# Seven-product blocks: partial sums that grow in PSUM, and quarter-weight sums made by adding transfers

## The chip, the cores and the metric

The kernel runs on one core of one Trainium2 chip. The metric is device microseconds (us) of one execution, the median over several runs. The engines are named as in the profile: PE (TensorE matmul), PEld (its weight load), DVE (VectorE), ACT (ScalarE), POOL (GpSimd) and SP (SyncE, which here only issues transfers). SBUF is the on-chip memory that all engines read and write; PSUM is the small memory into which PE adds up its products.

## The reference, cut to what matters

One layer of a hybrid model is computed for 1152 tokens (1024 of a prompt and 8 x 16 of a sample) with 1024 channels. The attention and the state-space scan in the middle are not touched by the change. It touches the three last matrix products, of which two are meant here: the attention projection and the output projection.

```python
att_branch = (o_att.reshape(b, s, ATT_WIDTH) * jax.nn.silu(z_att)) @ w_att_proj     # 1024 x 1024
...
ssd_branch = y @ w_ssd_proj                                                         # 2048 x 1024
g_att, g_ssd = jnp.split(gates, 2, axis=-1)
merged = jax.nn.sigmoid(g_att) * att_branch + jax.nn.sigmoid(g_ssd) * ssd_branch
out = x + gate * (merged @ w_out)                                                   # 1024 x 1024
```

## The kernel before, in words

Everything lies with channels on the 128 partitions and tokens along the columns. A matrix product in float32 precision is made of float16 parts: an operand x is split into hi = x rounded to float16 (made on ACT) and lo = x - hi (made on DVE), and a product is hi*hi + hi*lo + lo*hi, three matmuls that add up in the same PSUM bank. `halves` (L637, L638) makes the two parts, `level` (L629) adds a sum of squares of the raw operand on ACT, from which a `verdict` at the end decides on the chip whether the general version has to run after all.

The two projections are done in blocks by a scheme with seven products instead of eight (as in Strassen's and Winograd's methods). A block takes two output tiles of 128 channels (o = 0, 1), both halves of the tokens (t = 0, 1, 576 tokens each) and inputs in pairs of 128-channel tiles (k = 0 to 3, e = 0, 1). So weights and inputs are 2 x 2 arrays of quarters. Four sums or differences of quarter weights and four of quarter inputs are made first; seven products of quarters follow, and sums of these give the four output quarters. There are eight blocks: four for the attention projection, with the four phases of the state-space projection (`ssd_dense`) behind them, and then four for the output projection.

- `job` lists the weight loads in the order of use; `w_ahead` (L619) loads them on SP's queue into three raw places of 1024 columns. `quad_split(i)` makes the float16 weights of block i: it takes its two raw tiles, makes the four sums on DVE (L661 to L664, 512 columns each) in two tiles u, splits w[0], u[0], half of w[1] and u[1], and calls `level` on the raw tiles. `w_next(i)` is called twice within block i and makes the weights of block i + 1 when there is room.
- `pieces` makes the four input sums (L2154 to L2157) and all float16 parts (L2140 on ACT, L2142 on DVE) of one pair of input tiles.
- `quad_dense` runs a block. `product(q, banks)` issues 4 x 2 x 3 = 24 matmuls (L782 to L784), each 128 x 128 weights by 288 columns, into two banks. The banks rotate over the three PSUM pools s (one place of two banks), g (three banks) and d (three banks), a fresh pair for each product. Products come in the order 0, 1, 5, 6, 4, 3, 2. ACT copies product 0 to SBUF (L817), and DVE adds the others to partial sums in SBUF (`joined`, L796). In the first block of each projection (`wide`) the products 0, 1 and 2 run together, k by k, since the inputs of the last k arrive late.
- `evict(o, t, y)` takes one output quarter from SBUF: for the attention projection it multiplies by a gate row (L2218), for the output it scales, adds x and stores it (L2308, L2311, L2312, L2313). `verdict()` is called in the last block, at evict(1,1).
- `gate_loads` (L2189) fetches the 16 gate rows from memory on SP's queue, up to five ahead of the one in use. POOL's queue carries stores, among them those of the gate rows (L1823), and POOL computes a small chain (from L1306).
- All places in SBUF come from one arena with fixed layouts (`L_TAIL` "T" are places of 1152 columns, `L_WQ` of 512 words for weights). `alloc` raises `NoSlot` if no place is free, and the generator that asked tries later.

The program is first emitted by generators, one per activity, and `run` interleaves these by their estimated time. Then `Order` puts every engine's instructions in a fixed order: it simulates the engines with a cost for each instruction (a transfer issued by POOL 0.56 us, plus 2.1 us and its bytes) and takes, on each engine, the earliest emitted instruction that is ready, of those that are ready with a margin first. On the chip each engine runs its list in this order and waits where an input is not there yet.

Of the kernel before, what the change touches and what calls it, by code (L numbers as in the profile page):

```python
# [16 lines left out]
P = 128  # L17
# [403 lines left out]
def trunk_kernel(ctx: ExitStack, tc: tile.TileContext, h, again):  # L421
# [217 lines left out]

    def quad_split(i):  # L640

        w_ahead()
        w = [wraw[j] for j in jobs[i]]
        bufs = []
        try:
            for _ in range(7):
                bufs.append(alloc(L_WQ, "w", 1024))
            for _ in range(2):
                bufs.append(alloc(L_TAIL, "T", 1024))
# [4 lines left out]
        u = bufs[7:]  # L654
        del bufs[7:]
        for j in jobs[i]:
            wraw.pop(j)
        a, b = ([x.ap.rearrange("p (k e m) -> p e k m", e=2, m=P)[:, e] for e in range(2)] for x in w)
        t = [x.ap.rearrange("p (e k m) -> p e k m", e=2, m=P)[:, e] for x in u for e in range(2)]
        halves(bufs[0].r, bufs[1].r, w[0].ap, SW)  # L660
        nc.vector.tensor_tensor(t[0], b[0], b[1], ALU.add)  # L661
        nc.vector.tensor_tensor(t[1], t[0], a[0], ALU.subtract)  # L662
        nc.vector.tensor_tensor(t[2], a[0], b[0], ALU.subtract)
        nc.vector.tensor_tensor(t[3], a[1], t[1], ALU.subtract)  # L664
        k4 = lambda x: x.rearrange("p (k m) -> p k m", m=P)
        halves(bufs[3].r, bufs[4].r, u[0].ap, SW)
        halves(k4(bufs[2].r[:, :512]), k4(bufs[2].r[:, 512:]), b[1], SW)
# [6 lines left out]
        nat = lambda k, e: slice((2 * k + e) * P, (2 * k + e + 1) * P)  # L674
        col = lambda k, e: slice((4 * e + k) * P, (4 * e + k + 1) * P)
        pick = {0: (bufs[0], bufs[1], nat, 0, 0), 1: (bufs[0], bufs[1], nat, 1, 1), 2: (bufs[5], bufs[6], col, 1, 1),
# [75 lines left out]
    for i in range(0, 8, 2):  # L752
        job(h["watt"][i], h["watt"][i + 1], quad=True)
# [4 lines left out]
    for i in range(0, 8, 2):  # L758
        job(h["wout"][i], h["wout"][i + 1], quad=True)

    HT = NT // 2
    HC = NT // 4

    def quad_dense(ops, evict, last=False, wide=False):

        i = widx[0]
        widx[0] += 1
        _, w = yield from w_wait(i)
        used, begun = {}, set()

        def product(q, banks, ks=range(4)):
            if q in begun:
                return
            for k in ks:
# [5 lines left out]
                for g, ps in enumerate(banks):  # L780
                    c = slice(g * HC, (g + 1) * HC)
                    nc.tensor.matmul(ps, wh, xh[:, c], start=k == 0, stop=False)  # L782
                    nc.tensor.matmul(ps, wh, xl[:, c], start=False, stop=False)  # L783
                    nc.tensor.matmul(ps, wl, xh[:, c], start=False, stop=k == 3)  # L784
                    yield 3 * 122.0
# [6 lines left out]
        def joined(t, banks, op):  # L792
            y = yield from walloc(L_TAIL, "T", HT)
            for g, ps in enumerate(banks):
                c = slice(g * HC, (g + 1) * HC)
                nc.vector.tensor_tensor(y.ap[:, c], t.ap[:, c], ps, op)  # L796
            return y

        def bank(n):
            if n % 3 == 0:  # L800
                x = pss.tile([P, 2, 512], F32, tag="s", name=nm("s"))
                return [x[:, g, :HC] for g in range(2)]
            if n % 3 == 1:
# [3 lines left out]
        b = bank(0)  # L807
        if wide:
            qs = (0, b), (1, bank(1)), (2, bank(2))
# [3 lines left out]
            begun.update((0, 1, 2))  # L813
        yield from product(0, b)
        s1 = yield from walloc(L_TAIL, "T", HT)
        for g, ps in enumerate(b):
            nc.scalar.activation(s1.ap[:, g * HC:(g + 1) * HC], ps, AF.Copy)  # L817
        if wide:
            p3 = yield from walloc(L_TAIL, "T", HT)
            for g, ps in enumerate(qs[2][1]):  # L820
                nc.scalar.activation(p3.ap[:, g * HC:(g + 1) * HC], ps, AF.Copy)
        b = qs[1][1] if wide else bank(1)
        yield from product(1, b)
        c = yield from joined(s1, b, ALU.add)
        yield from evict(0, 0, c) or ()
        b = bank(2)
        yield from product(5, b)
# [3375 lines left out]
```

## Time and profile before

| | |
|---|---|
| time, median of 3 runs | 1734.88 us (1734.16 to 1736.05) |
| span of the profiled execution, first to last instruction | 1732.7 us |
| mean granted clock of TensorE | 0.998 |
| PE busy | 1706.9 us (99%) |
| DVE, ACT, POOL busy | 1294.7, 982.9, 314.4 us (75%, 57%, 18%) |
| transfers | 287.26 MB, mean 166 GB/s |

The profile is of one execution. Its own time outside the span is not recorded; the span stands 2.2 us below the median of the runs. In the groups, "x48 | 19.9, 450 | 20.4" means 48 instructions, 19.9 us busy in all, 450 ns each, and 20.4 us in which the engine was idle just before one of them, with what ended that idleness behind the arrow. In the timeline the first number is the start in us and the second the duration; matmuls overlap, so 0.29 us each are issued every 0.12 us.

### The profile page before, as it was taken

What the parts mean: (1) busy time and instruction counts of PE and PEld (TensorE: products, weight loads), DVE (VectorE), ACT (ScalarE), POOL (GpSimd) and SP (SyncE); (2) the same over time, 40 slices, a digit from 0 to 9 for tenths busy, and PEclk for the clock granted to TensorE, in tenths of its full rate; (3) what the DMA queues carried; (4) which work ended last, traced back from release to release, by engine and by line L of the source; (5) the groups of instructions that cost most, each with busy time, mean ns of one, the idle gap of its engine ahead of it and who ended that gap; (6) DMA issues with size and microseconds to landing.
All of it is one profiled execution on the core that took longest, in us unless ns stands there. A gap on an engine that the chain in (4) does not pass through costs nothing. (4 is left out here: it accounts for less than half of the span.)

```text
span 1732.7 us, 35395 instructions
## 1 busy us (share of the span) xinstructions
PE 1706.9 (99%) x13977; PEld 1094.3 (63%) x13977; DVE 1294.7 (75%) x2449; ACT 982.9 (57%) x1931; POOL 314.4 (18%) x576
## 2 busy tenths in 40 slices
PE   7999999999999999999999999999999999999998
PEld 3556566566555566667666666666666677666676
DVE  6458767878776876587869777777777878897694
ACT  8766556566465646566556545755567543365340
POOL 0243233225134011111311231112112200000000
PEclk9999999999999999999999999999999999999999
DMA  9248789887978586445655445544556646331141
GB/s 383 80 126 206 174 229 214 183 228 192 214 210 197 150 203 140 138 137 150 150 153 155 139 134 162 169 136 118 152 174 223 252 157 226 118 127 51 53 160 71
DMA packets 276777, 287.26 MB, mean 166 GB/s; under 512 B 209069, under 2 KB 209721, under 8 KB 276601
## 3 DMA queue, kind: packets, MB, share of 16 engines
q1 hardware_dynamic: 267640, 256.26, 53.7%
q0 software_dynamic: 8960, 28.65, 4.5%
q8 instruction: 111, 1.82, 0.5%
q14 instruction: 66, 0.53, 0.1%
HBM read 192.70 MB, written 43.66 MB: 136 GB/s over the span
## 5 line engine op out<-in xcount | busy, mean ns | idle before, releaser
L873 PE MATMUL d<-arena 128*128 128x384 f16 x1872 | 610.9, 326 | 2.8 <-ACT arena L1707 1.4
L876 PE MATMUL d<-arena 128*128 128x384 f16 x1872 | 610.3, 326 | 0.0
L874 PE MATMUL d<-arena 128*128 128x384 f16 x1872 | 610.3, 326 | 0.0
L873 PEld LDWEIGHTS <-arena 128*128 128x128 f16 x1896 | 185.5, 98 | 127.6 <-issue 13.6
L876 PEld LDWEIGHTS <-arena 128*128 128x128 f16 x1896 | 185.5, 98 | 122.6
L874 PEld LDWEIGHTS <-arena 128*128 128x128 f16 x1896 | 185.6, 98 | 117.2 <-issue 3.2
L629 ACT ACTIVATE arena<-arena 128x1024 bf16<-128x1024 f32 (+4 forms) x185 | 184.9, 999 | 106.1 <-DMA arena<-in_wall_dram 64.8
L638 DVE SCALAR_TENSOR_TENSOR arena<-arena 128x1024 f16<-128x1024 f32 (+2 forms) x133 | 159.6, 1205 | 75.5 <-ACT arena L637 72.7
L637 ACT ACTIVATE arena<-arena 128x1024 f16<-128x1024 f32 (+2 forms) x133 | 135.7, 1022 | 90.8 <-DVE arena L662 18.7
L926 PE MATMUL d<-arena 128*128 128x384 f16 (+1 forms) x568 | 186.8, 329 | 0.0
L928 PE MATMUL d<-arena 128*128 128x384 f16 (+1 forms) x568 | 186.1, 328 | 0.0
L927 PE MATMUL d<-arena 128*128 128x384 f16 (+1 forms) x568 | 186.1, 328 | 0.0
L1472 ACT ACTIVATE arena<-arena 128x640 f32<-128x640 f32 (+4 forms) x144 | 100.8, 701 | 62.7 <-DVE arena L1475 62.2
L1918 ACT ACTIVATE arena<-arena 128x128 f32<-128x128 f32 x288 | 89.4, 392 | 39.5 <-DMA arena<-acs_d 38.8
L1730 DVE SCALAR_TENSOR_TENSOR arena<-arena 128x1176 f32<-128x1176 f32 x72 | 104.0, 1445 | 3.3 <-issue 1.3
L926 PEld LDWEIGHTS <-arena 128*128 128x128 f16 x576 | 56.3, 98 | 50.8 <-issue 17.5
L1508 DVE SCALAR_TENSOR_TENSOR arena<-arena 128x640 f16<-128x640 f32 (+4 forms) x128 | 86.8, 711 | 0.0
L1367 ACT ACTIVATE arena<-d 128x256 f32<-128x256 f32 x71 | 26.9, 378 | 96.4 <-PE d L928 96.4
L928 PEld LDWEIGHTS <-arena 128*128 128x128 f16 x576 | 56.4, 98 | 38.4 <-issue 0.2
L927 PEld LDWEIGHTS <-arena 128*128 128x128 f16 x576 | 56.4, 98 | 32.8
L1475 DVE CUSTOM_DVE_ANT_0 arena<-s,arena 128x320 f32<-128x320 f32 (+4 forms) x128 | 60.2, 501 | 19.8 <-PE s L1637 9.8
L1400 POOL TENSOR_SCALAR arena<-arena 128x16 f32<-128x16 f32 (+1 forms) x24 | 10.0, 417 | 353.8 <-DVE arena L1373 353.6
(267 smaller groups left out, 3051.7 us busy)
## 6 DMA issues: line engine op xcount, KB each, us to landing
arena<-in_wall_dram SPq DMA_DIRECT2D x85, 512.0 KB, 4.7
arena<-acs_d SPq DMA_DIRECT2D x32, 576.0 KB, 4.7
arena<-in_kc_dram SPq DMA_DIRECT2D x64, 256.0 KB, 4.3
arena<-in_vc_dram SPq DMA_DIRECT2D x64, 256.0 KB, 4.6
arena<-in_wada_dram SPq DMA_DIRECT2D x24, 512.0 KB, 9.4
arena<-in_xT_dram SPq DMA_DIRECT2D x16, 576.0 KB, 6.7
gate_d<-arena POOLq DMA_DIRECT2D x48, 192.0 KB, 3.7
arena<-eacs_d SPq DMA_DIRECT2D x32, 288.0 KB, 5.5
```

The source lines that it names most:

```text
L629: keep(nc.scalar.activation(junk[:, :n], x, AF.Square, scale=scale * n ** -0.5, accum_out=sums[:, c:c + 1]))
L637: keep(nc.scalar.activation(hi, x, AF.Copy, scale=scale))
L638: keep(nc.vector.scalar_tensor_tensor(lo, x, scale, hi, ALU.mult, ALU.subtract))
L873: nc.tensor.matmul(ps, hi.r[:, wc], kh.r[:, tok], start=k == 0, stop=False)
L874: nc.tensor.matmul(ps, hi.r[:, wc], kl.r[:, tok], start=False, stop=False)
L876: nc.tensor.matmul(ps, lo.r[:, wc], kh.r[:, tok], start=False, stop=k == nk - 1)
L926: nc.tensor.matmul(ps, kh.r[:, tok], wh, start=k == 0, stop=False)
L927: nc.tensor.matmul(ps, kh.r[:, tok], wl, start=False, stop=False)
L928: nc.tensor.matmul(ps, kl.r[:, tok], wh, start=False, stop=k == KT - 1)
L1472: nc.scalar.activation(p, p, AF.Exp, bias=sm_[:, 4 + e:5 + e], scale=-1.0, accum_out=sm_[:, 6 + e:7 + e])
L1730: nc.vector.scalar_tensor_tensor(yc, r.ap[:, j:j + n], w4[:, i, j:j + 1], yc, ALU.mult, ALU.add)
L1918: nc.scalar.activation(me[e].ap[:, cs], me[e].ap[:, cs], AF.Relu, scale=-1.0, bias=a4[:, c, hds[e]:hds[e] + 1])
```

## The change

Three things change together in the blocks of seven products.

1. Partial sums stay in PSUM. Product 5 is added by PE onto the banks of product 0 (`first=False`: its first matmul does not clear the bank), 6 onto those, 3 onto those, and 2 onto the banks of product 4. Between two of these, ACT copies what is in the banks so far to SBUF (`kept`), or DVE adds them to such a copy (`joined`, now in place). The order becomes 0, 4, 5, 1, 6, 2, 3; in the wide blocks 0, 4, 1 together, then 5, 2, 6, 3. The last quarter, (1,0), is evicted straight from PSUM in two halves of 288 columns. To make all joins additions, some signs are turned: two input sums become scalar_tensor_tensor, the output of odd tiles is negated, and the state-space eviction and the output scaling account for it. `evict` now takes a list of pieces (start, width, tile).
2. The four sums of quarter weights come from memory. Weights are also laid out by quarters (`qatt`, `qout`). `quad_sums(i)` takes the two tiles u, loads one quarter into each of their four halves on SP's queue, and adds further quarters by seven adding transfers on POOL's queue (`accum_op=ALU.add`). It is called by `quad_split(i)`, and by `w_next(i)` for block i + 2.
3. `gate_loads` keeps three rows ahead instead of five, and the verdict is called at evict(0,1).

```diff
+    def gather(out, x):
+        nc.gpsimd.dma_start(out, x, accum_op=ALU.add)
+
+    wsums = {}
+
+    def quad_sums(i):
+        if i in wsums or i not in quads:
+            return
+        u = []
+        try:
+            for _ in range(2):
+                u.append(alloc(L_TAIL, "T", 1024))
...
+        (a11, a12), (a21, a22) = ([parts[j][:, e * 512:(e + 1) * 512] for e in range(2)] for j in jobs[i])
+        for x, y in zip(u, (a22, a11)):
+            for e in range(2):
+                dma(x.ap[:, e * 512:(e + 1) * 512], a21)
+            for e in range(2):
+                gather(x.ap[:, e * 512:(e + 1) * 512], y)
+        for x, y in ((u[0], a11), (u[1], a22), (u[1], a12)):
+            gather(x.ap[:, 512:], y)
+        wsums[i] = u
+
     def quad_split(i):
+        quad_sums(i)
         w_ahead()
...
         halves(bufs[0].r, bufs[1].r, w[0].ap, SW)
-        nc.vector.tensor_tensor(t[0], b[0], b[1], ALU.add)
-        nc.vector.tensor_tensor(t[1], t[0], a[0], ALU.subtract)
-        nc.vector.tensor_tensor(t[2], a[0], b[0], ALU.subtract)
-        nc.vector.tensor_tensor(t[3], a[1], t[1], ALU.subtract)
+        halves(bufs[2].r[:, :512], bufs[2].r[:, 512:], w[1].ap[:, 512:], SW)
         halves(bufs[3].r, bufs[4].r, u[0].ap, SW)
-        halves(k4(bufs[2].r[:, :512]), k4(bufs[2].r[:, 512:]), b[1], SW)
         halves(bufs[5].r, bufs[6].r, u[1].ap, SW)
...
     def w_next(i, keep=lambda x: x):
-        if w_left(i + 1):
-            try:
+        try:
+            if w_left(i + 1):
                 w_split(i + 1, keep)
-            except NoSlot:
-                pass
+            if i in quads:
+                quad_sums(i + 2)
+        except NoSlot:
+            pass
...
-        job(h["watt"][i], h["watt"][i + 1], quad=True)
+        job(h["qatt"][i], h["qatt"][i + 1], quad=True)
...
-        def product(q, banks, ks=range(4)):
+        def product(q, banks, ks=range(4), first=True):
...
-                    nc.tensor.matmul(ps, wh, xh[:, c], start=k == 0, stop=False)
+                    nc.tensor.matmul(ps, wh, xh[:, c], start=first and k == 0, stop=False, skip_group_check=not first)
...
-        def joined(t, banks, op):
+        def kept(banks):
             y = yield from walloc(L_TAIL, "T", HT)
             for g, ps in enumerate(banks):
+                nc.scalar.activation(y.ap[:, g * HC:(g + 1) * HC], ps, AF.Copy)
+            return y
+
+        def joined(y, banks):
+            for g, ps in enumerate(banks):
                 c = slice(g * HC, (g + 1) * HC)
-                nc.vector.tensor_tensor(y.ap[:, c], t.ap[:, c], ps, op)
-            return y
+                nc.vector.tensor_tensor(y.ap[:, c], y.ap[:, c], ps, ALU.add)
+            return [(0, HT, y.ap[:, :HT])]
...
+        fore = bank(2 if odd else 0)
+        side = bank(1)
         if wide:
+            lone = bank(0 if odd else 2)
             for k in range(4):
-                for q, x in qs:
+                for q, x in ((0, fore), (4, side), (1, lone)):
                     yield from product(q, x, (k,))
...
+        yield from product(0, fore)
+        p1 = yield from kept(fore)
+        yield from product(4, side)
+        p5 = yield from kept(side)
+        yield from product(5, fore, first=False)
+        u2 = yield from kept(fore)
+        if not wide:
+            lone = bank(0 if odd else 2)
+        yield from product(1, lone)
+        yield from evict(0, 0, joined(p1, lone)) or ()
+        p1.free()
         w_next(i)
         if wide:
+            yield from product(2, side, first=False)
+        yield from product(6, fore, first=False)
+        yield from evict(1, 1, joined(p5, fore)) or ()
+        p5.free()
+        if not wide:
+            yield from product(2, side, first=False)
+        yield from evict(0, 1, joined(u2, side)) or ()
+        u2.free()
+        w_next(i)
+        yield from product(3, fore, first=False)
+        yield from evict(1, 0, [(g * HC, HC, ps) for g, ps in enumerate(fore)]) or ()
         w_done(i)
...
-            yield from ready(lambda: len(gates) < gone[0] + 5)
+            yield from ready(lambda: len(gates) < gone[0] + 3)
...
-                if c == 6 and (o, t) == (1, 1):
+                if c == 6 and (o, t) == (0, 1):
                     verdict()
```

More of the change, by code (lines that the diff above doesn't have):

```diff
@@ L822, in quad_dense @@
[L822 to L827, printed above, removed]
-        u2 = yield from joined(s1, b, ALU.add)
-        s1.free()
-        b = bank(3)
-        yield from product(6, b)
-        u3 = yield from joined(u2, b, ALU.add)
-        w_next(i)
-        b = bank(4)
-        yield from product(4, b)
-        c = yield from joined(u3, b, ALU.add)
@@ L837, in quad_dense @@
[L837 to L844 removed]
+            begun.update((0, 4, 1))
+        yield from product(0, fore)
[3 more added lines that the diff above has]
+        yield from product(5, fore, first=False)
```

97 lines of the change are left out of this document (38 added, 59 removed).

## The prediction

> **What bounds the kernel now.** I read the page first (busy shares), then the stretches of the last part, where all the edits lie, then what TensorE waited for there, then the end of the timeline. Page, parts 1 and 2:
>
> ```profile
> span 1732.7 us, 35395 instructions
> PE 1706.9 (99%) x13977; PEld 1094.3 (63%) x13977; DVE 1294.7 (75%) x2449; ACT 982.9 (57%) x1931; POOL 314.4 (18%) x576
> ```
>
> TensorE is the bound: 25.8 us of the span without it. The stretches say where these are (columns: stretch, its length, busy us of PE, PEld, DVE, ACT, POOL with instruction counts, granted clock, DMA share, GB/s):
>
> ```profile
> 0.00:50.00 50.00, 38.59 (x285) 21.17 (x286) 35.85 (x52) 41.83 (x69) 0.85 (x8) 1.00 0.93 364
> 50.00:1330.00 1280.00, 1274.32 (x10903) 804.49 (x10902) 943.43 (x1892) 764.87 (x1595) 299.73 (x547) 1.00 0.63 167
> 1330.00:1366.00 36.00, 36.00 (x251) 21.94 (x248) 34.04 (x43) 27.20 (x46) 7.36 (x12) 1.00 0.68 238
> 1366.00:1455.00 89.00, 88.20 (x723) 68.19 (x722) 67.05 (x116) 35.39 (x56) 6.48 (x10) 1.00 0.50 172
> 1455.00:1642.00 187.00, 187.00 (x1152) 112.59 (x1151) 150.22 (x218) 89.49 (x130) 0.00 (x0) 1.00 0.34 114
> 1642.00:1725.00 83.00, 82.77 (x678) 65.94 (x675) 62.35 (x128) 24.11 (x39) 0.00 (x0) 1.00 0.33 116
> 1725.00:1733.00 8.00, 0.00 (x0) 0.00 (x0) 1.74 (x6) 0.00 (x0) 0.00 (x0) 0.61 0.14 50
> ```
>
> The four attention-projection blocks are 1366 to 1455, the four output blocks 1642 to 1725. In these two stretches PE lacks 0.80 and 0.23 us; behind them stands an end of 8 us without PE. The list of waits from 1366 on has one PE row, and a stretch of 20 us inside the output blocks gives the rate:
>
> ```profile
> PE s L782 <- ACT arena L817: 0.8, 1, 0.8
> 1680.00:1700.00 20.00, 20.00 (x166) 15.98 (x164) 14.23 (x31) 3.46 (x5) 0.00 (x0) 1.00 0.34 119
> ```
>
> 20 us for 166 matmuls is 0.1205 us each, at a granted clock of 1.00: a product (4 x 2 x 3 = 24 matmuls) takes 2.89 us, a block of seven 20.2 us. So whatever the edits save on DVE or ACT buys nothing by itself; they count through stalls of PE that they add or remove, and through the end.
>
> **The change, part by part.**
>
> *Matmuls.* Seven products of 24 before, seven after, same shapes. Cost 0, no cover needed.
>
> *Joins and copies.* Groups from 1350 on, and the forms of ACT from 1340 on (xcount | busy us, mean ns | idle before):
>
> ```profile
> L664 DVE TENSOR_TENSOR arena<-arena 128x512 f32<-128x512 f32 x8 | 5.5, 684 | 0.0
> L796 DVE TENSOR_TENSOR arena<-arena,g 128x288 f32<-128x288 f32 x48 | 19.9, 450 | 20.4 <-ACT arena L817 13.8 <-PE g L784 5.2 <-PE g L1011 1.3
> L2218 DVE SCALAR_TENSOR_TENSOR arena<-arena 128x576 f32<-128x576 f32 x16 | 12.1, 754 | 0.2
> L637 ACT ACTIVATE arena<-arena 128x1024 f16<-128x1024 f32 x40 | 42.0, 1054 | 73.4 <-DVE arena L662 18.7 <-DMA arena<-in_wssd_dram 12.1 <-PE d L874 11.8
> L638 DVE SCALAR_TENSOR_TENSOR arena<-arena 128x1024 f16<-128x1024 f32 (+1 forms) x47 | 52.8, 1128 | 4.1 <-PE d L874 2.0 <-ACT arena L637 2.0
> L817 ACT ACTIVATE arena<-s 128x288 f32<-128x288 f32 x16 | 5.7, 407 | 31.8 <-PE s L784 31.8
> ```
>
> DVE loses four sums of 0.684 and eight of fourteen joins of 0.450 per block: 2.7 + 3.6 = 6.3 us, about 50 us over eight blocks. Worth 0: no PE row waits for DVE there. ACT gains four copies of 0.407 in a plain block (six instead of two), 28 in all, 11.4 us; it is busy 35.39 of 89 and 24.11 of 83 us, so there is room: 0. If that room were gone, each copy would stand on PE's path with its 0.4 us.
>
> *Growing sums.* This is a new wait: product 5 may write the bank of product 0 only when ACT has copied it, 6 the bank of 5 only after its copy, 3 the bank of 6 only after DVE's join. In a plain block one other product lies between, 2.89 us of cover. A pair of copies runs 0.7 us (row below), a pair of joins 0.9. Behind one level (1.06 us, also below) the copies are done 1.8 us after the product: covered. Behind two of ACT's 1.05 us instructions it is 2.8, which leaves nothing for the steps between engines. I take 0 for the plain blocks, bounds 0 and 0.3 per handoff, 24 handoffs. In the two wide blocks the products 0, 4, 1 run together, so that only 12 matmuls (1.45 us) lie between the end of 0 and the start of 5, and there the present queue of ACT is close:
>
> ```profile
> 1646.31 3.89 DVE L2142 SCALAR_TENSOR_TENSOR arena<-arena 128x1152 f16<-128x1152 f32 x3
> 1649.36 1.06 ACT L629 ACTIVATE arena<-arena 128x1024 bf16<-128x1024 f32 x1
> 1650.42 0.69 ACT L817 ACTIVATE arena<-s 128x288 f32<-128x288 f32 x2
> ```
>
> The first output block starts at 1642.0; 54 + 6 matmuls later, at about 1649.2, product 0 is done, 5 may start at 1650.7, and the copies end at 1651.1. That is +0.3 us (bounds 0 and 0.5). The same block now wants product 4's fourth operand at 1649.2, where product 1's stood. It is the second of the three pieces made at L2142, ready at 1646.31 + 2 x 1.30 = 1648.9: just covered; 0.
>
> *Sums by transfers.* Per block: 4 plain loads and 7 adding transfers of 128 x 512 x 4 bytes = 256 KB, 2.9 MB, 23 MB in all. They are queued (POOL 7, SP 4 issues) and, an adding transfer having to see the earlier one landed, serial: the first tile is load, add, add; the second load, add, add, add. Only then follow ACT's 1.05 and DVE's 1.13 us of splitting, 2.3 with the step between them. The landing times from 1340 on, and what POOL's queue looks like beforehand:
>
> ```profile
> arena<-gate_d SPq DMA_DIRECT2D x15, 576.0 KB, 7.0
> out_y_dram<-arena SPq DMA_DIRECT2D x16, 288.0 KB, 3.2
> gate_d<-arena POOLq DMA_DIRECT2D x8, 192.0 KB, 5.5
> 1362.74 0.36 POOL L1306 TENSOR_SCALAR arena<-arena 128x9 f32<-128x9 f32 x1 [5.85 <-DMA arena<-ya]
> 1371.28 1.70 POOL L1823 DMA_DIRECT2D gate_d<-arena  x3
> ```
>
> No adding transfer is in this trace. I bound one by 3.2 and 7.0 us and take 5.0, nearest to POOL's own 5.5 with less weight on the crowded minutes. The issues cost 7 x 0.54 (a third of 1.70) = 3.8 us of POOL per block; after 1373 POOL has nothing else. Before that a waiting add holds up the gate stores L1823 and the chain from L1306; PE, by its one row above, never waited for either: 0, and at the worst the length of one landing. The loads of the sums are asked two blocks ahead for blocks 3 and 4 of each kind: over 20 us of lead against 4 x 7 = 28 at the worst and 20 at my value: 0. Blocks 1 and 2 have less:
>
> ```profile
> 1348.03 0.69 DVE L661 TENSOR_TENSOR arena<-arena 128x512 f32<-128x512 f32 x1
> 1375.71 0.69 DVE L661 TENSOR_TENSOR arena<-arena 128x512 f32<-128x512 f32 x1
> 1392.48 0.71 ACT L817 ACTIVATE arena<-s 128x288 f32<-128x288 f32 x2 [2.43 <-PE s L784]
> SPq L2189 <- DVE arena L796: 12.2, 2, 9.5
> ```
>
> The sums begin at L661. Block 2's did so at 1375.7; its product 0 ended at 1392.4. If the loads go out when L661 did (the gate loads L2189 waited up to 9.5 us for a tile that a join still used, so places are scarce there and much earlier is not sure), the first tile is summed at +3 x 5 = 1390.7 and split at 1393.0. Product 4 wants it at 1392.4, or at 1395.3 if 1, which needs raw quarters alone, goes first. The second tile is summed at 1395.7 and split at 1398; product 6 wants it after four products, 1401. So 0 to 0.6 us, and I take 0.3. The ends: with 3.2 us a landing nothing; with 7.0 the split is at 1399.0 and 1406, a stall of 4 to 6.6 us. Block 1's sums stood at 1348.0 and are wanted at about 1366.7: 1365.3 at 5.0, 1371.3 at 7.0, so 0, at the worst 4.6. The output blocks see a DMA share of 0.33 instead of 0.50: 0, at the worst 2.
>
> The Trainium skill's page "DMA: Bandwidth & Descriptors" (Anatomy of one DMA — SWDGE (gpsimd) path) fits a transfer issued by GpSimd as 2.0 us plus bytes over 436e3, by which an estimate for 256 KB is 2.6 us; the 5.5 us of 192 KB here disagree, and by 2.6 the stall in this step would be 0 and the time 1734.2. Its section "Rules for kernel authors" has it that an accumulating transfer must wait for the earlier one's semaphore, which speaks against this change, since three or four landings then come one after the other; no run here shows it yet.
>
> *Gates held to three ahead instead of five.* A gate row is asked at the start of its block and used by evict(1,1) five products later, 14.5 us against a landing of 7.0: 0; without that cover up to 7 us once, where the state-space blocks begin.
>
> *Signs, halved evictions.* The two operand sums that become scalar_tensor_tensor cost the same (0.754 per 576 columns at L2218), one 36-element scaling becomes two: 0, under PE.
>
> *The end.* The last lines of the timeline, and of the branch behind the program:
>
> ```profile
> 1719.37 0.18 DVE L2282 TENSOR_SCALAR arena<-g 128x32 f32<-128x32 f32 x1
> 1722.30 0.35 DVE L2291 TENSOR_REDUCE arena<-arena 128x1 f32<-128x195 f32 x1
> 1724.37 0.29 PE L784 MATMUL s<-arena 128*128 128x288 f16 x1
> 1724.69 0.46 DVE L796 TENSOR_TENSOR arena<-arena,s 128x288 f32<-128x288 f32 x1 [1.32 <-PE s L784]
> 1725.06 0.14 DVE L2294 TENSOR_SCALAR again<-g 1x1 int32<-1x1 f32 x1
> 1725.13 0.43 DVE L796 TENSOR_TENSOR arena<-arena,s 128x288 f32<-128x288 f32 x1
> 1725.60 0.69 DVE L2308 SCALAR_TENSOR_TENSOR arena<-arena 128x448 f32<-128x448 f32 x1
> 1726.20 0.28 DVE L2311 TENSOR_TENSOR arena<-arena 128x128 f32<-128x128 f32 x1
> 1726.52 0.29 DVE L2312 TENSOR_TENSOR arena<-arena 128x128 f32<-128x128 f32 x1
> 1726.84 0.34 SPq L2313 DMA_DIRECT2D out_y_dram<-arena  x1
> L4058 SPq EVENT_SEMAPHORE  x8: 17/17/17, 1730.5 to 1731.0; - x8
> ```
>
> From PE's end (1724.66) to the last store's issue are 2.18 us of DVE; SP's way out follows 3.6 us after that issue. Afterwards the last product is 3, evicted straight from its two banks by two 288-column instructions (0.45 each), the first beside the last matmuls: issue at 1725.3, which is -1.5. But the verdict (eleven small DVE instructions, L2282 to L2291, about 0.2 us each, 2.2 in all) now starts one product before the end instead of two, beside the 2.1 us of evict(0,1) (0.87 + 0.69 + 0.28 + 0.29). Those, the verdict and 0.9 for the two last evictions make 5.2 us; from 1721.8, where product 2 would end, that is 1727.0, or 1726.4 since successive instructions overlap by some 0.08 (L2308 and L2311 do): -0.4. I take -1.0, between the two.
>
> **Sum.** -1.0 (end) + 0.3 (wide handoff) + 0.3 (block 2's sums) = -0.4 us: 1732.7 becomes 1732.3. The median shown, 1734.88, stands 2.2 us above this span, for what lies around the first and last instruction; with it 1734.5. About 0.2%, 3.5 us, is what a measurement here can tell from no change, so this is "same".
>
> **Rivals.**
> *Late sums (slower).* The chain of loads and adds is longer than 5 us a link, and ACT, which takes its instructions in a fixed order, sits on a split whose tile has not landed; the copies behind it are late, and PE with them. For: places are scarce, the window 1366 to 1455 already moves 172 GB/s and gets 3 blocks' worth (8.6 MB) more, each add reads its target too. Against: PE has one product to put ahead, the output blocks have an idle DMA. It decides from about 6.2 us a link, where block 2's first tile is split at 1396.6, 4.2 us past its need, and the 0.7 us that the rest of the sum gains no longer hold the result within 3.5. With 7.0: 4.6 + 6.6 + 2, less what block 1's delay gives block 2 (a stall shifts the next need as well), 4 to 9 us net: 1738.5 to 1743.5, middle 1741. In the two blocks of each kind and with ACT blocked behind it, up to 13 us, 1747.
>
> *Handoffs not covered (slower).* ACT stands behind two long instructions at most handoffs: 24 x 0.3 = 7.2 us, 1741.7. For: at 1649.36 a level stands directly ahead of the copies. Against: at 40% and 29% load most copies find it free.
>
> *Faster by more than noise.* All that PE lacks from 1366 on is 1.03 us, and the end gives at most 1.5: 2.5 us or 0.14%. 1732.3 is the floor unless the order of instructions in the first 1366 us, where PE lacks 11.4 + 5.7 us, changes as well: 1731.
>
> **How the numbers follow.** Forecast 0.60 (own range 1732.3 to 1737.5: the floor, and half of a late tile), late sums 0.25, handoffs or gates 0.10, faster 0.05. So faster 0.05, same 0.60, slower 0.35. The range is 1732.0 to 1744.0: the forecast's and most of the late sums up to one bad link, leaving out some 4% below and 12% above.
>
> **What would show it.** Right: PE's 1366 to 1455 and 1642 to 1725 stretches still lack about 1 us; the adds land in 4 to 6 us; L664 is gone; the last store goes out 0.7 to 1.8 us after PE's end. Wrong: rows "PE <- ACT" at the copies of several us, and "ACT <- DMA" at the splits just before them (late sums); many such PE rows of 0.1 to 0.5 us without the DMA rows (handoffs); DVE's evictions waiting for gate_d (gates); POOL rows waiting for DMA while gate stores stand behind them. The forecast fails if an add costs much more than a load of the same size.

## The result, and the profile after

The changed kernel takes 1775.99 us (median of 4 runs, 1774.9 to 1779.37) against 1735.47 us (1734.16 to 1736.22) for the kernel before on the same chip: a ratio of 1.0233, 95% interval 1.0220 to 1.0246. It is 40.5 us slower; the forecast was 1734.5 us with a range up to 1744.0. The profiled execution has a span of 1774.3 us, 41.6 more than before. Two kernels below had one execution each, of 1828.59 and 3013.29 us, far above their others, which the ratios leave out (the medians don't) and for which no trace shows a cause.

The page and the stretches of the last part, as shown of the kernel before (in the stretches: length, busy us of PE, PEld, DVE, ACT, POOL, granted clock, DMA share, GB/s):

```profile
span 1774.3 us, 35494 instructions
PE 1715.3 (97%) x13977; PEld 1096.8 (62%) x13977; DVE 1254.1 (71%) x2363; ACT 990.8 (56%) x1959; POOL 360.3 (20%) x632
```

```profile
1330.00:1366.00 36.00, 29.57 (x240) 18.76 (x238) 24.18 (x33) 15.62 (x26) 11.72 (x16) 0.98 0.89 267
1366.00:1455.00 89.00, 82.57 (x628) 60.34 (x628) 50.56 (x74) 48.10 (x80) 21.27 (x30) 0.93 0.86 251
1642.00:1685.00 43.00, 43.00 (x316) 30.68 (x314) 26.51 (x41) 19.28 (x36) 6.09 (x7) 1.00 0.45 130
1685.00:1767.00 82.00, 63.03 (x478) 47.86 (x476) 31.02 (x68) 15.39 (x28) 12.16 (x14) 0.90 0.65 163
```

The number of matmuls is the same, yet PE is busy 8.4 us longer; the clock column says why. PE lacks 6.4 us from 1330 to 1366, 6.4 from 1366 to 1455 (4.4 of them the rest of a stall that began at 1359.6), and 19.0 in the last 82 us, of which 3.2 lie behind the last product. DVE has lost 40.6 us (some 50 were forecast), and nothing came of it. The waits from 1330 on (engine, tile, line, releaser: us in all, times, longest):

```profile
PE d L884 <- ACT arena L1833: 10.8, 1, 10.8
PE s L805 <- ACT arena L818: 6.2, 1, 6.2
PE g L805 <- ACT arena L637: 5.8, 1, 5.8
PE d L805 <- DVE arena L2322: 3.2, 1, 3.2
PE s L805 <- DVE arena L824: 2.0, 1, 2.0
PE g L807 <- DVE arena L638: 0.6, 1, 0.6
ACT arena L637 <- DMA arena<-in_qatt_dram: 33.4, 7, 9.1
ACT arena L637 <- DMA arena<-in_qout_dram: 27.9, 6, 11.9
POOL arena L641 <- DMA arena<-in_qatt_dram: 49.3, 11, 7.6
POOL arena L641 <- DMA arena<-in_qout_dram: 40.3, 14, 6.0
```

Six PE rows make 28.7 us of stall (a seventh, of 0.5, comes after the last product), where before there was one of 0.8. None of them names a transfer. PE waits for ACT and DVE; ACT (L637, a split) waits for transfers from the weights, 61.3 us in the two rows, of which 51.1 are for adding transfers (the list of who waited for L641); the rest is for raw tiles. POOL (L641, the issue of the adds) waits for the loads and adds before. One pass through it, at 1359 to 1370, on ACT and then on PE:

```profile
1355.48 0.48 ACT L1305 ACTIVATE arena<-g 96x384 f32<-96x384 f32 x1
1358.77 1.06 ACT L637 ACTIVATE arena<-arena 128x1024 f16<-128x1024 f32 x1 [2.81 <-DMA arena<-in_qatt_dram]
1368.93 1.06 ACT L637 ACTIVATE arena<-arena 128x1024 f16<-128x1024 f32 x1 [9.10 <-DMA arena<-in_qatt_dram]
1369.89 0.47 ACT L1833 ACTIVATE arena<-d 128x384 f32<-128x384 f32 x1
```

```profile
1359.25 0.33 PE L887 MATMUL d<-arena 128*128 128x384 f16 x1
1370.41 0.48 PE L884 MATMUL d<-arena 128*128 128x384 f16 x1 [10.84 <-ACT arena L1833]
```

In this stall, the longest, the matmuls that stop are not those of the blocks at all (in the other five rows they are): L884 is an ordinary product whose banks wait for the gate eviction L1833, a 0.47 us instruction with nothing wrong about it, except that it stands in ACT's list behind a split whose tile has not landed. The clock by 4 us around this stall (busy PE, clock, DMA share, GB/s) shows the second bill:

```profile
1358.00:1362.00 4.00, 1.57 (x10) 1.00 1.06 348
1362.00:1366.00 4.00, 0.00 (x0) 0.78 1.07 326
1366.00:1370.00 4.00, 0.00 (x0) 0.50 1.10 288
1370.00:1374.00 4.00, 3.58 (x12) 0.50 0.97 219
1374.00:1378.00 4.00, 4.00 (x25) 0.94 1.03 260
```

The clock falls to 0.5 in the stall and stays there for some 4 us after PE goes on: 12 matmuls in 3.6 us instead of 25 in 4. The Trainium skill (page "TensorE: Matmul & The Clock Gate", "Part 1: The HAM clock gate") says that the clock halves after an idle window of about 3.4 us and comes back after as long a busy one. This stall agrees. The one of 2.0 us that ends at 1448.9 is shorter than that window and was followed by 3.4 us at 0.50 all the same; there the measurement decides:

```profile
1447.00:1449.60 2.60, 0.68 (x6) 1.00 0.50 76
1449.60:1453.00 3.40, 3.40 (x16) 0.50 0.90 227
```

The packets, MB and share of 16 engines' span of the software queue (POOL's), before and after, and then the adding transfers by their line (issues, in ns and with first and last start; ACT's waits for them; landings):

```profile
q0 software_dynamic: 8960, 28.65, 4.5%
```

```profile
q0 software_dynamic: 17024, 43.33, 9.2%
```

```profile
L641 POOL DMA_DIRECT2D arena<-in_qatt_dram x28: 856/891/1943, 1289.0 to 1448.7; - x28
L641 POOL DMA_DIRECT2D arena<-in_qout_dram x28: 862/862/1571, 1602.8 to 1729.3; - x28
  ACT arena L637: 51.1, 9
DMA to landing us min/median/max: 3.6/6.2/13.5
```

An adding transfer lands 6.2 us after its issue in the median (3.6 to 13.5; from 1320 on 7.5 for the attention weights, 6.1 for the output weights) and costs POOL 0.89 us (0.86 for the output weights). The 56 of them take 9.2% x 1774.3 - 4.5% x 1732.7 = 85 us of all 16 DMA engines, about 1.52 us each.

So the 41.6 us of span are: stalls from 1330 on 28.7 - 0.8 = 27.9; slower matmuls after them 8.4; the end, from the last product to the last instruction, 10.7 instead of 8.1, 2.6; and 2.7 before 1330, which other runs with adding transfers don't all show.

### The profile page after: what moved, and what is told of

The parts are those of the page before. It is cut to its first block, busy times and chain, and to the rows that moved or that the text cites. A ratio compares the mean times of both kernels' runs of the same rounds, so it can differ in the third digit from the quotient of the medians.

```text
span 1774.3 us, 35494 instructions
## 1 busy us (share of the span) xinstructions
PE 1715.3 (97%) x13977; PEld 1096.8 (62%) x13977; DVE 1254.1 (71%) x2363; ACT 990.8 (56%) x1959; POOL 360.3 (20%) x632
## 4 chain that ended last, share of the span: by engine, by line
PE 77%; DMA 8%; DVE 5%; ACT 5%; issue 3%; POOL 1%; SPq 1%; POOLq 0%; ACTq 0%; DVEq 0%
PE d L884 15%; PE d L885 14%; PE d L887 14%; PE d L937 5%; PE d L939 5%; PE d L938 5%; DMA arena<-in_qatt_dram 3%; DMA arena<-in_qout_dram 2%; PE g L1543 2%; PE s L2004 2%; PE g L1976 1%; PE s L1590 1%; PE g L2024 1%; PE g L1590 1%; PE g L1678 1%
## 5 line engine op out<-in xcount | busy, mean ns | idle before, releaser
L884 PE MATMUL d<-arena 128*128 128x384 f16 x1872 | 611.8, 327 | 14.2 <-ACT arena L1833 10.8
L884 PEld LDWEIGHTS <-arena 128*128 128x128 f16 x1896 | 185.7, 98 | 128.0 <-issue 14.3
L637 ACT ACTIVATE arena<-arena 128x1024 f16<-128x1024 f32 (+1 forms) x133 | 135.5, 1021 | 119.1 <-DMA arena<-in_qatt_dram 34.3
L641 POOL DMA_DIRECT2D arena<-in_qout_dram x28 | 24.3, 940 | 256.4 <-DVE arena L638 154.7
```

The costliest lines, as they stand in the source:

```text
L637: keep(nc.scalar.activation(hi, x, AF.Copy, scale=scale))
L884: nc.tensor.matmul(ps, hi.r[:, wc], kh.r[:, tok], start=k == 0, stop=False)
```

## The experiments

Theories. *Late sums*: the chain of adding transfers is late, and POOL and ACT, in their fixed order, carry the delay on. *Handoffs*: the sums that grow in PSUM make PE wait for copies. *Crowding*: 23 MB more, or POOL's longer work, slow everything, whoever waits. All ratios are to the kernel before on the same chip; "adds" are adding transfers.

| kernel | median us | ratio (95%) |
|---|---|---|
| changed | 1775.99 | 1.0233 (1.0220 to 1.0246) |
| PSUM alone, weight sums on DVE | 1739.82 | 1.0029 (1.0019 to 1.0039) |
| same, gates 5 ahead, verdict earlier | 1737.56 | 1.0010 (1.0001 to 1.0019) |
| same, and a free bank for L1028 | 1736.19 | 0.9994 (0.9984 to 1.0003) |
| adds alone, sums kept in SBUF | 1802.45 | 1.0377 (1.0359 to 1.0395) |
| adds made, splits don't wait for them | 1763.72 | 1.0157 (1.0140 to 1.0174) |
| loads only, no adds | 1739.04 | 1.0018 (1.0009 to 1.0028) |
| plain transfers for adds, SP, chained | 1743.41 | 1.0034 (1.0023 to 1.0045) |
| slow plain transfers, SP, chained | 1753.49 | 1.0098 (1.0081 to 1.0114) |
| plain transfers, POOL, chained | 1758.84 | 1.0126 (1.0109 to 1.0143) |
| four adds a block instead of seven | 1769.91 | 1.0198 (1.0182 to 1.0215) |
| plain transfers, POOL, into memory, early | 1749.72 | 1.0067 (1.0049 to 1.0086) |
| plain transfers, POOL, not chained | 1743.18 | 1.0043 (1.0029 to 1.0057) |
| adds, order planned with true costs | 1764.23 | 1.0162 (1.0146 to 1.0177) |
| adds, late stores off POOL | 1784.69 | 1.0265 (1.0245 to 1.0286) |

**Half the change each.** PSUM alone:

```diff
-        halves(bufs[3].r, bufs[4].r, u[0].ap, SW)        # u loaded and added to by transfers
+        nc.vector.tensor_tensor(t[0], a21, a22, ALU.add)  # and three more like it, on raw tiles
+        halves(bufs[3].r, bufs[4].r, u[0].ap, SW)
```

> The changed kernel, but the four sums of quarter weights are made again by four DVE sums of 512 columns (0.68 us each) on the raw tiles; sums growing in PSUM, signs, gates three ahead and the verdict's place are kept. Late sums (the chain of loads and adding transfers, with POOL and ACT held in a fixed order behind it, costs all of the 40 us): 1733 to 1737 us, no gap of PE over 1 us after 1350 us. Handoffs (the growing sums make PE wait for copies): 1742 us or more, with many PE rows of 0.1 to 0.5 us at the copies. If the longer way out after PE's last product (10.6 instead of 8.1 us) comes from the adding transfers it is back at about 8 us here or below.

It is 1.0029, between the two. There is no row at a copy, so ACT's handoffs are covered, but there are two PE stalls at joins, and DVE's timeline has their cause:

```profile
PE s L811 <- DVE arena L830: 1.7, 1, 1.7
PE g L1028 <- DVE arena L830: 1.7, 1, 1.7
```

```profile
1386.82 1.42 DVE L2223 SCALAR_TENSOR_TENSOR arena<-arena 128x1152 f32<-128x1152 f32 x1 [8.22 <-DMA arena<-yb]
1388.15 0.81 DVE L830 TENSOR_TENSOR arena<-arena,g 128x288 f32<-128x288 f32 x2
1394.67 0.45 DVE L830 TENSOR_TENSOR arena<-arena,s 128x288 f32<-128x288 f32 x1
```

DVE stands 8.2 us at L2223 for a transfer of the state-space part, and the joins (L830) are behind it; L1028 is a small product of the output's modulation, which takes a g bank, and the growing sum holds two of the three g banks for five products. The other stall (L811) is a handoff: product 3 of the first block writes the s banks of product 6, and starts at 1395.18, when DVE has joined them. DVE came late to that as well, behind a second L2223 that waited 2.5 us. The next two kernels follow this up: first the gate limit and the verdict as before, then also the tile of L1028 in the d bank that the blocks leave free.

```diff
-            yield from ready(lambda: len(gates) < gone[0] + 3)
+            yield from ready(lambda: len(gates) < gone[0] + 5)
-                if c == 6 and (o, t) == (0, 1):
+                if c == 6 and (o, t) == (1, 1):
```

> Growing sums in PSUM with the weight sums on DVE (as in the run with PSUM alone), and besides the gate rows again five ahead and the verdict again at evict(1,1). If the 5 us that PSUM alone lost come from the gate rows' three-ahead limit (a load of the state-space row stands behind another that waits for a place, and DVE in its order behind that): 1733 to 1736 us. If they come from banks that are held longer: 1738 to 1741 us. The verdict's place should be worth at most 0.5 us.

```diff
-            ps, p2 = pg(), pg(36)
+            ps, p2 = pg(), psd.tile([P, 36], F32, tag="d", name=nm("d"))
```

> Growing sums in PSUM with the weight sums on DVE, gate rows five ahead, verdict at evict(1,1), and the small PSUM tile of the output's modulation (L1028 writes it) in the third d bank, which the blocks leave free, instead of a g bank, of which the growing sum holds two of three. If the 1.4 to 1.7 us that PE waited there are most of what PSUM alone lost: the wait is gone and the time is 1733.5 to 1736.5 us, level with before or up to 0.1% faster for the shorter end. If the loss lies in many small handoffs: 1737 us or more, as without this edit.

The first gains some 3 of the 5 us (limit and verdict weren't tried apart), with 1.4 us at L1028 still there and the clock at 0.76 to 0.80 for 8 us behind it. With the free bank that row is gone, one of 1.2 us at another join is left, and the time is that of the kernel before: 0.9994, no difference that can be told. The step between these two kernels is of the size of their intervals, and their profiled spans are alike (1736.1 and 1736.2 us), so what the bank alone is worth is not shown. Growing sums are worth nothing here, and in the last form they cost nothing.

The other half, with a fresh bank for each product, one copy and the joins in SBUF:

> The changed kernel, but partial sums are kept in SBUF as before: a fresh pair of banks for each product, ACT copies product 0, DVE does the joins; product order 0, 1, 5, 6, 4, 3, 2; verdict at evict(1,1). The sums by adding transfers stay. Late sums: 1765 to 1785 us, with PE gaps of several us behind splits that wait for transfers. Handoffs: 1733 to 1740 us. If both matter, between 1745 and 1765 us.

The adds make the loss, and without the growing sums it is even larger than expected, 1.0377. So the two halves of the change don't add up: with growing sums the adds cost less. Why is not shown. Joins in SBUF need more places, and POOL stood up to 42.1 us at an add whose place a join still held, but in the changed kernel that was 36.0 us too.

**Is it the waiting split?** The two splits of the summed tiles read raw tiles instead:

```diff
-        halves(bufs[3].r, bufs[4].r, u[0].ap, SW)
+        halves(bufs[3].r, bufs[4].r, w[1].ap, SW)
```

> The changed kernel with all loads and adding transfers issued as they are, but the two splits of the summed tiles read the raw tiles in their place (so the sums are made and not used). Late sums: ACT and DVE no longer stand before a tile that has not landed; PE loses what it lost only where a place is still held by an unfinished add: 1734 to 1742 us. Traffic (23 MB more, and POOL's queue crowded, slow everything): the gaps stay, 1765 us or more. The way out after PE's last product stays near 10.6 us if the adding transfers as such lengthen it.

Both expectations missed: 1.0157, so about a third of the loss hangs on the splits' waiting and two thirds doesn't. SP's waits from 1330 on, and one of ACT's, say what else a late sum holds:

```profile
SPq L2313 <- DMA arena<-in_qout_dram: 39.0, 6, 10.8
SPq L660 <- DMA arena<-in_qout_dram: 19.6, 4, 6.9
SPq L2200 <- DMA arena<-in_qatt_dram: 17.8, 4, 9.8
```

```profile
ACT arena L637 <- DMA arena<-in_qatt_dram: 19.2, 4, 7.9
```

Loads of x (L2313) and of gate rows (L2200) wait for places in which a sum is still being made, and SP's queue with them; the second fence is ACT waiting for raw tiles, the only ones of these weights that L637 reads here. A tile that nobody reads yet delays others by the place it takes; how much of the two thirds that makes, and how much POOL's order, no run separates.

**Links of the chain.** Four kernels keep loads, places and splits, and change what follows the loads: nothing at all; plain transfers of the same bytes instead of adds, on SP's queue or on POOL's (each still waits for the one before, into the same place); or only the first four adds (two of the four sums then lack three terms in all). In all of them the weights' sums lack terms.

```diff
-        nc.gpsimd.dma_start(out, x, accum_op=ALU.add)
+        nc.sync.dma_start(out, x)                      # plain, SP
+        nc.gpsimd.dma_start(out, x)                    # plain, POOL
```

> The changed kernel without its adding transfers: the four plain loads of quarters a block stay, two blocks ahead and into the same places, and the splits wait for them (so a first term stands where the sum of quarters would). Late sums, if the chain of adds on POOL's queue is what is late: 1738 to 1742 us, as with sums on DVE, and the way out after PE's last product is about 7 us again instead of 10 to 13. If places held by the early tiles and four more loads a block on SP's queue are enough: 1755 us or more.

> As the run with plain transfers in place of the adding ones (1758.8 us), but issued on SP's queue; the chain into the same place stays, three or four landings one after the other. If POOL's queue (issue of 0.9 us, landing of 5 to 6 us, other work held in its order) is what costs: 1738 to 1748 us. If the chain of landings costs, on whichever queue: 1755 us or more; SP then holds up the raw loads behind each waiting link as well.

> The changed kernel with each of the seven adding transfers a block replaced by a plain transfer of the same bytes on the same queue into the same place (so the last one written stays instead of the sum); each still has to wait for the one before. If it is the price of adding that makes the chain late (landing 6.1 to 7.5 us against 3.8 to 4.5 us for a plain load of the same size): links of about 4 us, 1735 to 1745 us. If it is the serial waits through POOL's queue whatever is transferred: 1760 us or more.

> The changed kernel with four adding transfers a block instead of seven: each half tile gets its load and one add, the longer chains are cut off (three of the sums lack terms). Late sums, in proportion to the links behind each other (a load and one add instead of a load and up to three): between the run without adds and the changed kernel, 1745 to 1760 us. If a single late link already does the whole harm: 1765 us or more.

Against the kernel before, loads, places and early requests cost 3 us; a chain of plain transfers on SP 6; the same chain on POOL 22, which neither of its expectations had, and where one transfer is issued in 0.54 us and lands in 5.3 (median); adds, with 0.89 and 6.2, 40. Of the 22 us, 5.4 are the end: 13.5 us from the last product to the last instruction, against 8.1 before and 7.7 with the chain on SP. Four adds already cost 34, as the second expectation of that run had it. The loss is not in proportion to the number of links; that fits a few late links doing most of it, but no run tells which. The queue table of the POOL run gives a plain transfer's time on the DMA engines, and its line the landings:

```profile
q0 software_dynamic: 13440, 43.33, 6.8%
```

```profile
DMA to landing us min/median/max: 2.8/5.3/9.4
```

6.8% x 1760.4 - 78.0 = 41.7 us for 56, about 0.75 us each: an add takes twice that, and in packets, from the same tables, 144 against 80. The Trainium skill (page "Collectives: The Full Stack", "The bandwidth ceiling: the fold count and why AG ≠ RS ≠ AR") has it of the reduction in a collective that its add needs two source reads where a copy has one; the factor of two here fits that, though no run shows the reads themselves.

**Engine time, or the chain?** Two more kernels. One makes SP's plain links slow, by reading 256 bytes at a time:

```diff
+        a11, a12, a22 = (parts[jobs[i][o]].rearrange("p (k e m) -> p k e m", e=2, m=64)[:, :, e] for o, e in ...)
-        nc.sync.dma_start(out, x)
+        nc.sync.dma_start(out.rearrange("p (k m) -> p k m", m=64), x)
```

> The run with plain chained transfers on SP's queue (1743.4 us), but the seven transfers read every second group of 64 columns (256 bytes at a time) of a twice as wide row, so that each should keep the DMA engines busy longer; chain, bytes and queue stay (other columns than the wanted ones are moved). If it is time on the DMA engines that makes an adding transfer dear: 1755 us or more, and the queue table shows at least 30 us of 16 engines more than the run with whole rows. If it is POOL's queue: within 4 us of that run, 1740 to 1748 us.

The hardware queue of the run before it, and its own:

```profile
q1 hardware_dynamic: 280888, 279.34, 56.5%
```

```profile
q1 hardware_dynamic: 331064, 279.34, 58.1%
```

The second is busy 58.1% of 1750.9 us, the first 56.5% of 1742.3; that is 33 us more, about 0.6 us for each of the 56 links, and the time rises by some 10 us, from 1.0034 to 1.0098: between the two expectations. Slower links cost, on SP too, but not as much as adds on POOL. The other leaves POOL its 56 transfers and takes the chain away. In a first form the planner issued them 180 us early and more, since nothing held them, so that its loss (a stall of 5.4 us at 1122, far from the blocks, and 5.8 us more at the end) says little:

> As the run with plain transfers on POOL's queue, but each of the seven writes a region of its own in memory that nobody reads or waits for; the four loads into the tiles stay and the splits wait for these alone (one term stands for the sum). Same number of issues and bytes on POOL's queue, no waiting between them. If waiting is what costs: 1738 to 1743 us, as with the loads alone (1739.0), plus up to 5 us for POOL's way out at the end. If POOL's issues and the traffic cost by themselves: 1755 us or more.

In the second each reads the half tile once its load has landed, and writes it to memory:

```diff
-        nc.gpsimd.dma_start(out, x, accum_op=ALU.add)
+        nc.gpsimd.dma_start(scr_d[nscr[0]], out)
```

> As the run with unchained transfers, but each of the seven on POOL's queue reads the half tile (after its load has landed) and writes a region of memory that nobody uses, so that they are issued when the sums would be and not long before; none waits for another, and the splits wait for the loads alone. If the chain of waits on POOL is what costs: 1739 to 1745 us plus up to 5 us for POOL's way out at the end. If issues, bytes and POOL's order cost as they are: near the chained plain transfers, 1755 us or more.

Its stretches of PE (busy, clock, DMA share, GB/s), and POOL's drains at the end of the program, before and in this run (shortest, median and longest in ns, first and last start):

```profile
1330.00:1366.00 36.00, 36.00 (x267) 1.00 0.91 316
1366.00:1455.00 89.00, 88.84 (x728) 1.00 0.76 274
1642.00:1725.00 83.00, 82.85 (x677) 1.00 0.58 213
```

```profile
L4185 POOLq DRAIN  x3: 40/107/1213, 1729.7 to 1732.5; - x3
```

```profile
L4209 POOLq DRAIN  x3: 40/107/5787, 1731.9 to 1738.2; - x3
```

This run decides the most. It has the same number of POOL issues and the same bytes, a DMA share of 0.91 and 0.76 in the first two stretches where the changed kernel has 0.89 and 0.86, and PE lacks 0.00, 0.16 and 0.15 us in the three. Its last product ends at 1724.85, that of the kernel before at 1724.66. So these issues and bytes by themselves cost PE nothing. All that this execution loses is the end: POOL's longest drain there lasts 5.8 us and reaches to 1737.7 (before: 1.2 us). It is the shortest of the five, 2.9 us under their median, and what the others lose besides is not recorded.

The run takes two waits away at once, that of a link for the one before and that of the splits for the links. Places are still waited for, SP up to 7.2 us for one that such a transfer reads. And a transfer here takes 0.66 us of the DMA engines (6.6% x 1738.5 - 78.0 = 36.8 us for 56), not an add's 1.52, so the adds' own engine time without a chain is in no run. With that said: issues and bytes are harmless to PE until something waits for them, and then the loss grows with what a link costs, 22 us for plain links on POOL and 40 for adding ones.

**The order.** First the planner is told what an add costs (0.9 us of POOL, 4 us more to land). Then the last gate and y stores go to SP's queue, out of POOL's order.

```diff
-            return 560.0 if e == "Pool" else 380.0, p * n * 4 / 360.0
+            return 900.0 if x.name in self.slow else 560.0 if e == "Pool" else 380.0, p * n * 4 / 360.0
-                lat = bus + 700 - t
+                lat = bus + 700 - t + 4000 * (u["ins"][0].name in self.slow)
```

> The changed kernel, but the planner of the instruction order counts an adding transfer as it was measured: 0.9 us of POOL instead of 0.56, and 4 us more until it has landed. It then plans an end of PE that is 7 us later than with its own numbers (1730.9 against 1724.0). If most of the 40 us come from ACT and POOL standing in an order that was planned with too short transfers: 1742 to 1755 us. If the chain itself cannot be made in time, whatever the order: 1760 us or more.

```diff
-            store(gate_d[i][:, tok], t.ap)
+            (dma if i >= 10 else store)(gate_d[i][:, tok], t.ap)
```

> The changed kernel with the last six gate rows' stores and the last three y stores issued on SP's queue, so that they no longer stand in POOL's order behind adding transfers that wait. If most of the loss in the attention blocks is made by these held stores (places that come free late, a gate eviction that waits 3.9 us for one): 1755 to 1765 us. If ACT's order behind the late sums makes it: 1770 to 1778 us, with the 10 us gap of PE near 1360 to 1370 still there.

With true costs the stall near 1360 shrinks from 10.8 to 2.8 us and the time to 1.0162: about 12 of 40 us were an order planned with transfers that were too short. The other 28 stay, so this better informed plan doesn't make the chain short enough. With the stores elsewhere the ratio is higher than either expectation, 1.0265, and the stall is 11.5 us: that these stores were held by POOL's order was not the cause.

## Why the prediction was wrong, step by step

- *What bounds, and what DVE's relief is worth*: right in kind. DVE falls from 1295 to 1272 us in the PSUM kernels and to 1254 in those that also drop the sums (40.6 us, where 50 were forecast), and none of them is faster than the kernel before.
- *Matmuls*: the count was right, but their cost is not fixed. PE's 8.4 us more are matmuls at half clock after a stall. The prediction had no such term. Over the five stalls of 2 us or more it is some 1.7 us for each, as an average.
- *Growing sums*: at ACT's copies 0 for the plain blocks and 0.3 for the wide ones hold, in that with PSUM alone no PE row stands at a copy. (By the row shown the copies end at 1651.1 and product 5 may start at 1650.7, which makes 0.4 and not 0.3; it changes nothing.) At DVE's joins the bound failed once: product 3 of the first block waited 1.7 us for the join of product 6, against at most 0.3, since DVE stood for a transfer of another part. What was overlooked besides is the bank that a growing sum holds: PSUM alone lost 5 us, 1.7 of it at L1028, which is no handoff, and with limit, verdict and bank changed nothing is lost.
- *Sums by transfers*: this is the step that failed; 0.3 us were counted for it, and 27.9 us of stall with 8.4 us of slow matmuls behind them were found. Three of its terms were off. (1) A link was put at 5.0 us between bounds of 3.2 and 7.0; it measured 6.2 in the median, 7.5 in the attention blocks, and 13.5 at worst, outside the bounds. A plain transfer on POOL measured 5.3: the nearest row was a fair price for a POOL transfer, and low for one that adds. The issue, put at 0.54 (a third of 1.70 is 0.57), measured 0.89. (2) Blocks 3 and 4 of each kind were put at 0, with over 20 us of lead, which by the prediction's own 28 us at the worst didn't cover them. Nor was the lead there: the sums were asked early, but went out when a place came free and POOL's list came to them. The loads for all output blocks but the first went out from 1667.5 on, after SP had waited up to 21.4 us for a place (23.9 in the unchained kernel, so that this wait is not made by the adds), and the last add at 1729.3, 34 us before the last product. In the output blocks, put at 2 us at worst, 15.8 us of stall are found. (3) A waiting add on POOL was put at 0, "at the worst the length of one landing". In the unchained kernel, where nothing waits for POOL's transfers but places, PE's loss is gone.
- *Late sums as a rival*: its mechanism is the one found, ACT in its order behind a split, and its threshold of 6.2 us a link is where the median was, by chance to the digit. Its price, 4 to 9 us or 13 at most, was too small because it was counted per late tile against that tile's own need. The stall of 10.8 us came before the blocks began, in a product that doesn't need the sums.
- *Gates, signs*: no stall of PE at a gate row is seen in the changed kernel; the gate limit may hold part of the 3 us between the first two PSUM kernels.
- *The end*: the last store goes out 0.9 us after PE's end (0.7 to 1.8 was forecast), 1.3 earlier than before. But that is not the end: from the last product to the last instruction it is 8.1 us before, 7.8 with PSUM alone, and 6.6 and 8.2 in the two kernels after it, so that the -1.0 is neither confirmed nor refuted. With the adds it is 10.7, and POOL's drain there is 3.4 us long instead of 1.2. With the loads alone it is 10.1, though, with a drain of 1.2 us (about 7 was expected), so the drain is not shown to make the difference.

What stays open: why four adds cost nearly as much as seven, what sets the end without adds, what the adds' engine time costs without a chain, and how the loss outside the splits divides between held places and POOL's order. The kernel without a chain shortens both at once.

## What to carry to other kernels

Ask of a transfer that takes over an engine's work not whether the queue has room but how many landings stand behind each other, and what else is written in the waiting engines' lists after the first reader: the longest stall appeared there, at an instruction that has nothing to do with the transfer. A chain of three or four landings needs its lead in places, not only in requests. And price a stall of the bound engine with what may follow it, a slow clock included.

## What the runs showed of the hardware

- An adding transfer of 256 KB keeps the DMA engines busy for about 1.52 us of all 16, a plain one for 0.75; it is issued in 0.89 us on POOL against 0.54 and lands in 6.2 against 5.3 us (medians, in chains). Plain ones on POOL from SBUF to memory, without a chain, landed in 6.0.
- The Trainium skill's fit for POOL's transfers (page "DMA: Bandwidth & Descriptors", "Anatomy of one DMA — SWDGE (gpsimd) path"), an estimate of 2.6 us for these bytes, lies below the shortest landing of an add here, 3.6 us, and of a plain one into SBUF, 2.8. The shortest of the plain ones to memory took 2.3 us. The medians are all at twice the fit and more.
- POOL's drain at the end of the program takes 1.2 us without the new transfers on its queue, 3.4 to 4.4 with 56 adds, and 5.8 with 56 plain ones, even where the last had been issued 48 us before.
- PE's clock went to half after a stall of 2.0 us, for 3.4 us. After the two stalls of 1.7 us with PSUM alone it stayed at 1.00.
